# Seven-product k groups in the middle of a pair, and in the out and down projections too

## The chip, the cores and the metric

The kernel runs on one core of one Trainium2 chip. The metric is the device time of one execution in microseconds (us), as a median over several runs. Engines are named as in the profile: PE is TensorE's matmul, PEld its weight load, DVE is VectorE, ACT ScalarE, POOL GpSimd, SP SyncE (here it only issues loads and stores). L494 is line 494 of the kernel before.

## The reference

A decoder trunk of two layers on 256 tokens of width 2048, in float32. Every large product has 256 rows (two tiles of 128 tokens) and a weight that is streamed once from memory.

```
h = h + mamba2_mixer(rmsnorm(h)) # z, x, B, C, dt by in_proj (2048 -> 10304); ends in y @ out_proj (4096 -> 2048)
h = h + swiglu(rmsnorm(h))       # g, u = split(h @ w_gate_up) (2048 -> 2 x 5632); (silu(g) * u) @ w_down (5632 -> 2048)
k, v, cum = shared_kv(h)         # 2048 -> 4112
h = h + forgetting_attention(rmsnorm(h), k, v, cum)   # w_q (2048 -> 2048), softmax, o @ w_o (2048 -> 2048)
h = h + swiglu(rmsnorm(h))       # w_gate_up and w_down of the second layer
```

## The kernel before

**Blocks, k groups, pieces.** A weight is cut into blocks of 512 columns (`NB`) and k groups of 512 rows (`KT` = 4 times 128). One block times one k group is a `Unit`, 1 MB, one load on SP into a `wraw` tile (`RAW` = 3 of these). Float32 is computed from two halves, high and low: ACT makes `whi` by a cast (L247), DVE makes `wlo` = raw - `whi` (L253), and PE runs three matmuls for each 128 x 512 of weight and each 128 tokens (high x high, high x low, low x high; L494 to L496). A unit is split in two pieces of 128 x 1024, each with 12 matmuls. The activations lie in slots, split in the same way (`xT`, one slot for each k group).

**What sets the order.** The program is recorded by `stream` in a fixed order, each engine's queue in that order. Before piece i is multiplied, `split_to(i + SPL)` with `SPL` = 4 puts the splits up to piece i + 3 on ACT and DVE; `whi` and `wlo` have 4 buffers each, so the cast of piece i + 3 waits until PE is done with piece i - 1. Work on results (adding into `h`, norms, transposes into the next slots) is written as generators in `Flow`, which puts it between the pieces by planned costs; `flow.finish` forces what is still open of a task into the queues at once.

**Products of sums.** In the gate and up projections (`ffn_up`, 22 pairs of a gate and an up block over both layers) one k group of four is multiplied as a 2 x 2 block matrix (k halves by gate/up, and k halves by token tile) with seven products in place of eight: `split_cross` and `cross_step`, in the order `Cross.ORDER` = d, g, a, c, e, b, f. A product is one piece of 6 matmuls (L410 to L412), so the group has 42 matmuls in place of 48. Its weight operands are made on DVE in place in the raw tiles (four additions of 128 x 1024, L365) and then split like any other. Of the seven, d, g and f read raw quarters or what was added for them; the additions for later products overwrite a quarter, so they stand behind the split that still reads it:

```
src = {"d": b21, "g": b11, "a": b21, "c": b22, "e": b21, "b": b22, "f": b12}[name]
```

The activation operands of a, c, e and f are sums too (`xS`, made in `sums_of`, L555 to L558, when the slot is filled). Before, the crossed k group is the last one, after the three plain ones of gate and then those of up; products g and b go on in the two PSUM tiles of gate (`acc`), f and a in those of up, d, c and e in tiles of a second pool of four (`mis`), which the transposes use as well. `inline` and `rest` (L617 and on, recorded from L624) combine the products on DVE.

**Out and down projections.** `out_stage` (out projection of either mixer, and down projection of layer 0) and the last loop (down projection of layer 1) run four blocks one after the other with `wide`, all k groups plain: 8 k groups in the Mamba out projection, 11 in the down projections, 4 in the attention's.

Of the kernel before, what the change touches and what calls it, by code (L numbers as in the profile page):

```python
# [9 lines left out]
F32 = mybir.dt.float32  # L10
# [7 lines left out]
P = 128  # L18
# [6 lines left out]
G = 8  # L25
# [9 lines left out]
KT = 4  # L35

# [56 lines left out]
class Flow:  # L93
# [70 lines left out]

class Slot:


    def __init__(self, summed=False):
        self.tile, self.task, self.summed, self.sums = None, None, summed, None
# [10 lines left out]
class Block:  # L180
# [3 lines left out]
    def __init__(self, xs, done, fills=None, wcol=None):  # L184
        self.xs, self.done, self.fills, self.wcol = xs, done, fills, wcol
        self.units, self.ps, self.task = [], None, None
        self.paired, self.stops = False, [KT * len(xs) - 1] * NT


class Cross:  # L190
# [7 lines left out]
    ORDER = "dgacebf"  # L198

    def __init__(self, left, right, units, x, inline, rest_of):  # L200
        self.left, self.right, self.units, self.x = left, right, units, x
        self.inline, self.rest_of = inline, rest_of
        self.ps, self.rest = {}, None
# [3 lines left out]
def kernel(ctx: ExitStack, tc: tile.TileContext, xT_d, x_d, cols_d, rows_d, wdt_d, win_d,  # L207
# [99 lines left out]
    def pair(xs, src_l, src_r, inline, rest, fills):  # L307


        both = []  # L310
        for src in (src_l, src_r):
            b = Block(xs, None, fills if src is src_r else None)
            b.paired = True
            if src is src_r:
                b.stops[1] -= KT
            for kg in range(len(xs) - 1):
                b.units.append(Unit(b, kg, src[kg].rearrange("p (k n) -> p k n", n=NB), NB, [[0, 1], [2, 3]]))
            blocks.append(b)
            both.append(b)
        last = [Unit(None, len(xs) - 1, src[len(xs) - 1].rearrange("p (k n) -> p k n", n=NB), NB, [list(range(KT))])  # L320
                for src in (src_l, src_r)]
        blocks.append(Cross(*both, last, xs[-1], inline, rest))
# [35 lines left out]
    def split_cross(x, name):  # L358
# [24 lines left out]
    def cross_step(x, name, parts):  # L383
# [3 lines left out]
        s = slot_of(x.x)  # L387
        left, right = x.left.ps, x.right.ps
        if name == "d":
            x.rest = phase.tile([P, NB], F32, tag="c4", name=nm("rest"))  # L390
            nc.scalar.copy(out=x.rest, in_=right[1])
            flow.work("A", 0.48)
        own = {"g": left[0], "b": left[1], "f": right[0]}
        if name in own:
            ps = own[name]
        elif name == "a":
            ps = right[1]
        else:
            ps = bank([P, NB])
        x.ps[name] = ps  # L400

        def a_of(part, p):
# [3 lines left out]
            return x.x.sums[:, "acef".index(name), part, p, :]  # L406

        for p in range(2):
            xh, xl = a_of(0, p), a_of(1, p)
            nc.tensor.matmul(ps, lhsT=xh, rhs=hi[:, p, :], start=p == 0 and name not in own, stop=False)  # L410
            nc.tensor.matmul(ps, lhsT=xh, rhs=lo[:, p, :], start=False, stop=False)
            nc.tensor.matmul(ps, lhsT=xl, rhs=hi[:, p, :], start=False, stop=p == 1)  # L412
        x.inline(x, name)
        if name == "b":
            x.left.task = Task(None, None)
            x.left.task.done = x.left.task.evac = True
        if name == "f":
            x.right.task = x.right.fills.task = spawn(x.rest_of(x))
# [3 lines left out]
    def stream(pre_load, pre_split):  # L422
        pieces = []
        for b in blocks:
            pieces += [(b, n) for n in Cross.ORDER] if isinstance(b, Cross) else [(u, ks) for u in b.units for ks in u.pieces]
        units = [u for b in blocks for u in b.units]
# [11 lines left out]
        def split_to(n):  # L438
            for i in range(len(parts), min(n, len(pieces))):
                u, ks = pieces[i]  # L440
                if isinstance(u, Cross):
                    parts[i] = split_cross(u, ks)
                    if ks in "ef":
                        load_to(units.index(u.units["ef".index(ks)]) + 1 + RAW)
# [10 lines left out]
        for i, (u, ks) in enumerate(pieces):  # L455
            if isinstance(u, Cross) and ks == "b":
                cross_step(u, ks, parts[i])
                split_to(i + SPL)
                continue
            split_to(i + SPL)  # L460
            if isinstance(u, Cross):
# [25 lines left out]
            if last or (b.paired and u.kg == 0 and ks[0] == 0):  # L487
                order = [(j, t) for t in range(NT) for j in range(len(ks))]
            for n, (j, t) in enumerate(order):
# [6 lines left out]
                nc.tensor.matmul(b.ps[t], lhsT=xl, rhs=hi[:, j, :], start=False, stop=k == b.stops[t])  # L496
# [3 lines left out]
            if last and not b.paired:  # L500
# [3 lines left out]
        for q in (flow.urgent, flow.mid, flow.lazy):  # L504
            while q:
                flow.finish(q[-1])
                q.popleft()
# [38 lines left out]
    def sums_of(dst, half, ps, wcol):  # L546

        if half == 0:
            dst.sums = slot([P, 4, 2, 2, P], F32R, "xS")
        y = tok("y").rearrange("p (f t) -> p f t", t=T)  # L550
        for f in range(2):
            nc.scalar.activation(y[:, f], ps[:, f, :], AF.Copy, scale=col(wcol + 2 * half + f))
        s = tok("xsum").rearrange("p (n t) -> p n t", t=P)
# [5 lines left out]
        yield A(0.72) + V(0.8)  # L559
        split(dst.sums[:, :, 0, half, :], dst.sums[:, :, 1, half, :], s)  # L560
        yield A(0.6) + V(0.6)

# [28 lines left out]
    def out_stage(xs, w_d, wcol, summed=False):  # L591

        ss = const.tile([P, NT, 4], F32, name=nm("ss"))
        nxt = [Slot(summed and j == 3) for j in range(4)]
# [671 lines left out]
```

## Time and profile before

| | before |
|---|---|
| runs | 2542.09, 2542.38, 2542.40 us, median 2542.38 us |
| profiled execution | 2543.43 us, of which span 2541.7 us |
| granted PE clock, mean | 0.999 |
| PE busy | 2526.5 us (99%), 11638 matmuls |
| PEld, DVE, ACT busy | 82%, 69%, 52% |
| HBM | 189 GB/s over the span |

The span is the time from the first to the last instruction of the profiled execution; the time of a run has some 1.7 us more. Matmuls are pipelined, so a row shows each with 0.39 us though the next starts 0.23 us later: what PE does in a stretch is read from starts, not from busy time.

### The profile page before, as it was taken

The page shows a single profiled execution, that of the slowest core. Times are in us where ns is not written, and L with a number is a line of the kernel's source. Part 1 is how long each engine was busy: PE and PEld are TensorE (multiplying, and loading weights), DVE is VectorE, ACT ScalarE, POOL GpSimd, SP SyncE. Part 2 cuts the span into 40 slices and gives each one's busy share as a digit, 9 for nine tenths or more (in the row PEclk, how much of TensorE's full clock was granted, in tenths as well). Part 3 has the DMA queues.
Part 4 walks back from the last instruction along what each step waited for, and adds up shares of the span by engine and source line. Part 5 has one row for each costly group of instructions (what it writes and reads, how often), then busy time and mean ns, then how long its engine had stood idle before and what let it go on. Part 6 is the DMA issues. An engine that isn't in the chain of part 4 may idle for free.

```text
span 2541.7 us, 29859 instructions
## 1 busy us (share of the span) xinstructions
PE 2526.5 (99%) x11638; PEld 2093.4 (82%) x11638; DVE 1742.4 (69%) x2227; ACT 1325.5 (52%) x1683; POOL 37.7 (1%) x52
## 2 busy tenths in 40 slices
PE   9999999999999999999999999999999999999999
PEld 7888888888888888888888888888888888888887
DVE  6777777755477878787444567775587887876444
ACT  6666565654455545454444556564555555544333
POOL 0000000000000000000000010000000000000000
PEclk9999999999999999999999999999999999999999
DMA  7655455445554655555555555445555564655664
GB/s 262 225 174 180 167 182 199 176 172 191 190 196 168 215 183 199 199 181 200 192 189 194 188 181 203 161 156 181 182 180 202 175 222 166 215 182 200 206 201 139
DMA packets 68317, 481.11 MB, mean 189 GB/s; under 512 B 7600, under 2 KB 8256, under 8 KB 10576
## 3 DMA queue, kind: packets, MB, share of 16 engines
q1 hardware_dynamic: 66672, 468.64, 53.1%
q0 software_dynamic: 1504, 10.57, 1.1%
q8 instruction: 91, 1.49, 0.2%
q14 instruction: 50, 0.41, 0.0%
HBM read 477.00 MB, written 2.18 MB: 189 GB/s over the span
## 4 chain that ended last, share of the span: by engine, by line
PE 90%; DVE 7%; ACT 2%; issue 1%; DMA 0%; SPq 0%; ACTq 0%; DVEq 0%
PE acc L494 28%; PE acc L496 28%; PE acc L495 28%; DVE wlo L253 3%; ACT whi L247 2%; PE mis L530 1%; DVE y L624 1%; PE mis L917 1%; DVE wraw L365 1%; DVE sg L624 1%; DVE d L624 1%; PE mis L787 0%; PE mis L923 0%; PE mis L1022 0%; PE mis L852 0%
## 5 line engine op out<-in xcount | busy, mean ns | idle before, releaser
L253 DVE TENSOR_TENSOR wlo<-wraw,whi 128x1024 fp32r<-128x1024 f32 (+1 forms) x851 | 1027.5, 1220 | 560.5 <-ACT whi L247 554.6
L247 ACT CAST whi<-wraw 128x1024 fp32r<-128x1024 f32 (+1 forms) x854 | 885.5, 1050 | 875.6 <-PE acc L496 790.5
L494 PE MATMUL acc<-whi,xT 128*128 128x512 f32 x3040 | 1196.7, 394 | 9.1 <-DVE y L624 6.8
L495 PE MATMUL acc<-wlo,xT 128*128 128x512 f32 x3040 | 1184.3, 390 | 1.0 <-DVE wlo L253 1.0
L496 PE MATMUL acc<-whi,xT 128*128 128x512 f32 x3040 | 1184.4, 390 | 0.0
L494 PEld LDWEIGHTS acc<-whi,xT 128*128 128x128 f32 x3040 | 571.2, 188 | 134.3 <-DVE y L624 16.1
L496 PEld LDWEIGHTS acc<-whi,xT 128*128 128x128 f32 x3040 | 571.1, 188 | 119.8
L495 PEld LDWEIGHTS acc<-wlo,xT 128*128 128x128 f32 x3040 | 571.6, 188 | 116.8 <-DVE wlo L253 1.6
L255 DVE SCALAR_TENSOR_TENSOR wlo<-wraw,cols,whi 128x512 fp32r<-128x512 f32 x192 | 134.6, 747 | 74.7 <-ACT whi L249 74.0
L249 ACT ACTIVATE whi<-wraw,cols 128x512 fp32r<-128x512 f32 x192 | 127.5, 717 | 73.9 <-PE acc L496 68.8
L253 DVE TENSOR_TENSOR xT<-mis,xT 128x512 fp32r<-128x512 f32 x52 | 33.5, 686 | 38.3 <-ACT xT L247 38.3
L247 ACT CAST xT<-mis 128x512 fp32r<-128x512 f32 x52 | 27.9, 589 | 54.5 <-PE mis L530 54.5
L365 DVE TENSOR_TENSOR wraw<-wraw 128x1024 f32<-128x1024 f32 x44 | 53.9, 1225 | 1.5
L365 DVE TENSOR_TENSOR wraw<-wraw,wraw 128x1024 f32<-128x1024 f32 x44 | 53.9, 1224 | 1.5
L517 POOL TENSOR_TENSOR rs<-ms,mhalf 128x4 f32<-128x4 f32 (+1 forms) x27 | 28.4, 1052 | 1503.2 <-DVE ms L515 1502.9
L494 PE MATMUL acc<-whi,oT 128*128 128x512 f32 x128 | 50.5, 394 | 0.0
L496 PE MATMUL acc<-whi,oT 128*128 128x512 f32 x128 | 49.9, 390 | 0.0
L495 PE MATMUL acc<-wlo,oT 128*128 128x512 f32 x128 | 49.8, 389 | 0.0
L249 ACT ACTIVATE xT<-mis,cols 128x256 fp32r<-128x256 f32 x64 | 25.5, 475 | 35.1 <-PE mis L530 35.1
L255 DVE SCALAR_TENSOR_TENSOR xT<-mis,cols,xT 128x256 fp32r<-128x256 f32 x64 | 26.8, 477 | 22.4 <-ACT xT L249 22.2
L800 DVE SCALAR_TENSOR_TENSOR xf<-mis,cols,xf 128x255 f32<-128x255 f32 (+2 forms) x96 | 39.7, 473 | 2.4 <-ACT xf L794 2.4
L410 PE MATMUL acc<-whi,xT 128*128 128x512 f32 x88 | 34.2, 389 | 0.0
(221 smaller groups left out, 1672.1 us busy)
## 6 DMA issues: line engine op xcount, KB each, us to landing
wraw<-in_gu_dram SPq DMA_DIRECT2D x176, 1024.0 KB, 4.8
wraw<-in_dn_dram SPq DMA_DIRECT2D x88, 1024.0 KB, 4.9
wraw<-in_win_dram SPq DMA_DIRECT2D x78, 1024.0 KB, 4.9
wraw<-in_wout_dram SPq DMA_DIRECT2D x32, 1024.0 KB, 4.8
wraw<-in_wq_dram SPq DMA_DIRECT2D x16, 1024.0 KB, 4.8
wraw<-in_wk_dram SPq DMA_DIRECT2D x16, 1024.0 KB, 4.8
wraw<-in_wv_dram SPq DMA_DIRECT2D x16, 1024.0 KB, 4.8
wraw<-in_wo_dram SPq DMA_DIRECT2D x16, 1024.0 KB, 4.8
```

The lines of the kernel that those rows point to most:

```text
L247: nc.scalar.copy(out=hi, in_=src)
L249: nc.scalar.activation(hi, src, AF.Copy, scale=scal)
L253: nc.vector.tensor_tensor(out=lo, in0=src, in1=hi.bitcast(F32), op=ALU.subtract)
L255: nc.vector.scalar_tensor_tensor(out=lo, in0=src, scalar=scal, in1=hi.bitcast(F32), op0=ALU.mult, op1=ALU.subtract)
L365: nc.vector.tensor_tensor(out=out, in0=in0, in1=in1, op=ALU.add)
L410: nc.tensor.matmul(ps, lhsT=xh, rhs=hi[:, p, :], start=p == 0 and name not in own, stop=False)
L494: nc.tensor.matmul(b.ps[t], lhsT=xh, rhs=hi[:, j, :], start=k == 0, stop=False)
L495: nc.tensor.matmul(b.ps[t], lhsT=xh, rhs=lo[:, j, :], start=False, stop=False)
L496: nc.tensor.matmul(b.ps[t], lhsT=xl, rhs=hi[:, j, :], start=False, stop=k == b.stops[t])
L517: nc.gpsimd.tensor_tensor(out=r, in0=ms, in1=mhalf[:, :width], op=ALU.pow)
L624: nc.vector.tensor_tensor(out=out, in0=in0, in1=in1, op=op)
L800: nc.vector.scalar_tensor_tensor(out=dst[:, i, s:], in0=pt[half][:, f, :T - s], scalar=col(w + 3 - s), in1=dst[:, i, s:], op0=ALU.mult, op ...
```

## The change

The crossed k groups become entries of a pair's common order. `pair` now alternates left and right units by k group and puts a `Group` where a k group is crossed; all products of a pair's crossed groups accumulate in the same seven PSUM tiles, d, a, e and c in four `mis` tiles of their own, and g, b and f in left's two tiles and right's first. They are combined once, at the last group (`parts`, `parts_to_h`). Gate and up have the crossed group at k group 2 of 0 to 3. The Mamba out projection crosses k groups 3 and 6 of 8 in both pairs (`WOUT`), the down projections 3 and 7 (`DN0`) and 3, 6 and 9 (`DN1`) of 11, the attention's out projection 2 of 4. That is 16 crossed groups more, 38 in all. The order of the products becomes d, g, a, e, c, b, f, and one addition moves with it from c to a. The sums for the activations of the new groups are made by `add_sums` from the two halves of a filled slot. Before the first group of a pair, `finish_all` forces all open work into the queues.

```
-    ORDER = "dgacebf"
+    ORDER = "dgaecbf"
...
+WOUT, DN0, DN1 = (3, 6), (3, 7), (3, 6, 9)
...
+    def finish_all(self):
+        for q in (self.urgent, self.mid, self.lazy):
+            while q:
+                self.finish(q[-1])
+                q.popleft()
...
+    def pair(xs, sources, done, fills, crossed, parts):
+        both = [Block(xs, d, f) for d, f in zip(done, fills)]
+        x = Cross(*both, parts)
+        order = []
+        for kg in range(len(xs)):
+            us = [Unit(b, kg, src[kg].rearrange("p (k n) -> p k n", n=NB), NB, [[0, 1], [2, 3]])
+                  for b, src in zip(both, sources)]
+            if kg in crossed:
+                order.append(Group(x, us, xs[kg], kg == crossed[0], kg == crossed[-1]))
+            else:
+                for b, u in zip(both, us):
+                    b.units.append(u)
+                order += us
+        blocks.append(order)
...
         split_hi(hi, src)
         if name == "g":
             add(b22, b12, b22)
-        if name == "c":
-            add(b21, b12, b21)
         split_lo(hi, lo, src)
         if name == "d":
             add(b21, b21, b22)
+        if name == "a":
+            add(b21, b12, b21)
         if name == "c":
             add(b22, b11, b21)
...
+        x, act = group.cross, group.x
+        s = slot_of(act)
+        if act.adder is not None:
+            flow.finish(act.adder)
+        own = {"g": x.left.ps[0], "b": x.left.ps[1], "f": x.right.ps[0]}
+        if group.first:
+            if name == "d":
+                flow.finish_all()
+            x.ps[name] = own[name] if name in own else bank([P, NB])
...
+        if group.last and name == "c":
+            spawn(x.parts(x))
...
-            if isinstance(u, Cross) and ks == "b":
-                cross_step(u, ks, parts[i])
-                split_to(i + SPL)
-                continue
             split_to(i + SPL)
-            if isinstance(u, Cross):
+            if isinstance(u, Group):
                 cross_step(u, ks, parts[i])
...
+    def add_sums(dst):
+        def run():
+            if not dst.task.done:
+                yield dst.task
+            s = dst.tile
+            for half in range(2):
+                y = tok("y").rearrange("p (f t) -> p f t", t=T)
+                part = [s[:, i, 2 * half:2 * half + 2, :].bitcast(F32) for i in range(2)]
+                nc.vector.tensor_tensor(out=y, in0=part[0], in1=part[1], op=ALU.add)
+                yield V(0.66)
+                yield from sums_from(dst, half, y)
+        dst.adder = spawn(run(), flow.mid)
...
+        def gate(x, ps):
+            for t, g in enumerate(x.part[:2]):
+                yield tt(g, ps[t], g)
...
-        for j in range(4):
-            wide(xs, w_d[j], done(j), nxt[j])
+        for j in (0, 2):
+            pair(xs, w_d[j:j + 2], (done(j), done(j + 1)), nxt[j:j + 2], crossed, parts_to_h(j))
```

What the change does to the queues, at three places. Numbers in names tell buffers apart; lines shift with the change (split L253 becomes L266, addition L365 becomes L378, combining L624 becomes L616).

DVE, the crossed group of the sixth gate/up pair of layer 0, before: `wraw_8505` holds the gate's unit (b11, b21), `wraw_8554` the up's (b12, b22). The splits (`wlo`) are those of d, g, a, c, e, b, and after `sg` that of f.

```order
L253 TENSOR_TENSOR wlo_8605<-wraw_8505,whi_8604 128x1024
L365 TENSOR_TENSOR wraw_8505<-wraw_8505,wraw_8554 128x2x512
L365 TENSOR_TENSOR wraw_8554<-wraw_8554 128x2x512
L253 TENSOR_TENSOR wlo_8622<-wraw_8505,whi_8621 128x1024
L253 TENSOR_TENSOR wlo_8639<-wraw_8505,whi_8638 128x1024
L365 TENSOR_TENSOR wraw_8505<-wraw_8554,wraw_8505 128x2x512
L253 TENSOR_TENSOR wlo_8655<-wraw_8554,whi_8654 128x1024
L365 TENSOR_TENSOR wraw_8554<-wraw_8505 128x2x512
L253 TENSOR_TENSOR wlo_8670<-wraw_8505,whi_8669 128x1024
L253 TENSOR_TENSOR wlo_8684<-wraw_8554,whi_8683 128x1024
L624 TENSOR_TENSOR sg_8693<-acc_8428,d_8681 128x512
L253 TENSOR_TENSOR wlo_8696<-wraw_8554,whi_8695 128x1024
```

The same engine in a crossed group of that stage with the change, `wraw_7886` the gate's and `wraw_7926` the up's unit; splits of d, g, a, e, c, b, f:

```order
L266 TENSOR_TENSOR wlo_7992<-wraw_7886,whi_7991 128x1024
L378 TENSOR_TENSOR wraw_7886<-wraw_7886,wraw_7926 128x2x512
L378 TENSOR_TENSOR wraw_7926<-wraw_7926 128x2x512
L266 TENSOR_TENSOR wlo_8009<-wraw_7886,whi_8008 128x1024
L266 TENSOR_TENSOR wlo_8026<-wraw_7886,whi_8025 128x1024
L378 TENSOR_TENSOR wraw_7886<-wraw_7926,wraw_7886 128x2x512
L266 TENSOR_TENSOR wlo_8043<-wraw_7886,whi_8042 128x1024
L266 TENSOR_TENSOR wlo_8054<-wraw_7926,whi_8053 128x1024
L378 TENSOR_TENSOR wraw_7926<-wraw_7886 128x2x512
L266 TENSOR_TENSOR wlo_8067<-wraw_7926,whi_8066 128x1024
L266 TENSOR_TENSOR wlo_8078<-wraw_7926,whi_8077 128x1024
```

The split of e now follows straight behind the addition that makes e's operand, and the split of b straight behind the addition that makes b's; before, another product's split stood in between at both places. The casts on ACT stand in the same order as the splits.

DVE around the end of a gate/up pair, before: `d`, `y` and `u` combine products, `acc_8429` is the gate's second PSUM tile, which the next pair's gate writes again; the splits are those of the next pair's first pieces.

```order
L253 TENSOR_TENSOR wlo_8696<-wraw_8554,whi_8695 128x1024
L253 TENSOR_TENSOR wlo_8709<-wraw_8590,whi_8708 128x1024
L624 TENSOR_TENSOR d_8681<-mis_8712,d_8681 128x512
L624 TENSOR_TENSOR y_8719<-mis_8701,d_8681 128x512
L624 TENSOR_TENSOR y_8719<-y_8719,acc_8429 128x512
L253 TENSOR_TENSOR wlo_8730<-wraw_8590,whi_8729 128x1024
```

And with the change, where the gate's tiles (`acc_7888`, `acc_7889`) are read while PE runs up's last unit, and up's (`acc_7928`, `acc_7929`) while it runs the next gate's first:

```order
L266 TENSOR_TENSOR wlo_8133<-wraw_8058,whi_8132 128x1024
L266 TENSOR_TENSOR wlo_8151<-wraw_8081,whi_8150 128x1024
L266 TENSOR_TENSOR wlo_8167<-wraw_8081,whi_8166 128x1024
L616 TENSOR_TENSOR d_8101<-acc_7888,d_8101 128x512
L616 TENSOR_TENSOR y_8103<-acc_7889,y_8103 128x512
L266 TENSOR_TENSOR wlo_8189<-wraw_8113,whi_8188 128x1024
L266 TENSOR_TENSOR wlo_8205<-wraw_8113,whi_8204 128x1024
L616 TENSOR_TENSOR v_8102<-acc_7928,v_8102 128x512
```

The last product's result moved away from the border of two pairs, by one unit of 24 matmuls on either side.

DVE at the first crossed group of the Mamba out projection, with the change: `wlo_4507` is the split of e, `wlo_4575` that of c. Between them stand four splits of `xT` (slot 7) and four times the six rows from L579 to L266 `xS`, two for slot 3 (`xS_4531`) and two for slot 6 (`xS_4550`); one of the four is shown.

```order
L266 TENSOR_TENSOR wlo_4507<-wraw_4343,whi_4506 128x1024
L268 SCALAR_TENSOR_TENSOR xT_4510<-mis_4511,cols,xT_4510 128x256 x2
L268 SCALAR_TENSOR_TENSOR xT_4510<-mis_4520,cols,xT_4510 128x256 x2
L579 TENSOR_TENSOR y_4529<-xT_3546 128x512
L562 TENSOR_TENSOR xsum_4532<-y_4529 128x128
L563 TENSOR_TENSOR xsum_4532<-y_4529 128x128
L564 TENSOR_TENSOR xsum_4532<-y_4529,xsum_4532 128x128
L565 TENSOR_TENSOR xsum_4532<-y_4529,xsum_4532 128x128
L266 TENSOR_TENSOR xS_4531<-xsum_4532,xS_4531 128x4x128
...
L266 TENSOR_TENSOR wlo_4575<-wraw_4400,whi_4574 128x1024
```

Before, there is only the filling of slot 7 at the same spot, between two plain splits:

```order
L253 TENSOR_TENSOR wlo_4470<-wraw_4341,whi_4469 128x1024
L255 SCALAR_TENSOR_TENSOR xT_4481<-mis_4482,cols,xT_4481 128x256 x2
L255 SCALAR_TENSOR_TENSOR xT_4481<-mis_4491,cols,xT_4481 128x256 x2
L253 TENSOR_TENSOR wlo_4507<-wraw_4398,whi_4506 128x1024
```

So 28 instructions came in between the split of e and that of c, which DVE runs in this order. At the first crossed group of the down projection of layer 1 the last slot's share of these stands at the same spot (one `xS` and two times six rows), at that of layer 0 one `xS`.

## Rows read from the trace of the kernel before

**Rows 1.** Page, part 1: busy time.

```profile
PE 2526.5 (99%) x11638; PEld 2093.4 (82%) x11638; DVE 1742.4 (69%) x2227; ACT 1325.5 (52%) x1683; POOL 37.7 (1%) x52
```

**Rows 2.** Waits of PE: total us, times, longest us.

```profile
PE acc L494 <- DVE y L624: 6.8, 22, 0.9
```

**Rows 3.** Timeline of PE in plain pieces: start us, duration, engine, line, [idle before].

```profile
1100.08 0.39 PE L494 MATMUL acc<-whi,xT 128*128 128x512 f32 x1
...
1108.24 0.39 PE L494 MATMUL acc<-whi,xT 128*128 128x512 f32 x1
```

**Rows 4.** Timeline of PE at the borders of gate/up pairs.

```profile
1138.15 0.39 PE L496 MATMUL acc<-whi,xT 128*128 128x512 f32 x1
1138.77 0.50 PE L494 MATMUL acc<-whi,xT 128*128 128x512 f32 x1 [0.23 <-DVE y L624]
1139.11 0.40 PE L495 MATMUL acc<-wlo,xT 128*128 128x512 f32 x1
...
1182.35 0.50 PE L494 MATMUL acc<-whi,xT 128*128 128x512 f32 x1 [0.91 <-DVE y L624]
...
1862.17 0.50 PE L494 MATMUL acc<-whi,xT 128*128 128x512 f32 x1 [0.58 <-DVE y L624]
```

**Rows 5.** Timeline of PE in one crossed group: d's first matmul, b's second.

```profile
1127.50 0.39 PE L410 MATMUL mis<-whi,xT 128*128 128x512 f32 x1
...
1134.52 0.39 PE L411 MATMUL acc<-wlo,xT 128*128 128x512 f32 x1
```

**Rows 6.** Timeline of ACT in and behind the same group: casts.

```profile
1125.02 1.05 ACT L247 CAST whi<-wraw 128x1024 fp32r<-128x1024 f32 x1 [1.71 <-PE acc L496]
...
1131.42 4.13 ACT L247 CAST whi<-wraw 128x1024 fp32r<-128x1024 f32 x4 [0.71 <-DVE wraw L365]
1137.37 2.00 ACT L247 CAST whi<-wraw 128x1024 fp32r<-128x1024 f32 x2 [1.82 <-DMA wraw<-in_gu_dram]
```

**Rows 7.** Timeline of DVE in the same group, from the split of a on.

```profile
1126.11 1.22 DVE L253 TENSOR_TENSOR wlo<-wraw,whi 128x1024 fp32r<-128x1024 f32 x1 [0.60 <-ACT whi L247]
1127.36 1.22 DVE L365 TENSOR_TENSOR wraw<-wraw,wraw 128x1024 f32<-128x1024 f32 x1
...
1130.09 1.22 DVE L365 TENSOR_TENSOR wraw<-wraw 128x1024 f32<-128x1024 f32 x1
1131.23 2.50 DVE L253 TENSOR_TENSOR wlo<-wraw,whi 128x1024 fp32r<-128x1024 f32 x2
```

**Rows 8.** DMA issues: operation xcount, KB each, median us to landing.

```profile
wraw<-in_gu_dram SPq DMA_DIRECT2D x176, 1024.0 KB, 4.8
```

**Rows 9.** Timeline of DVE and ACT, operations on slots and sums.

```profile
554.00 1.66 DVE L255 SCALAR_TENSOR_TENSOR xT<-mis,cols,xT 128x256 fp32r<-128x256 f32 x4
...
707.66 0.84 ACT L249 ACTIVATE xT<-mis,cols 128x256 fp32r<-128x256 f32 x2 [2.11 <-PE mis L530]
...
710.32 0.29 DVE L555 TENSOR_TENSOR xsum<-y 128x128 f32<-128x128 f32 x1 [0.91 <-ACT y L552]
...
711.05 0.29 DVE L558 TENSOR_TENSOR xsum<-y,xsum 128x128 f32<-128x128 f32 x1
...
711.38 0.62 ACT L247 CAST xS<-xsum 128x512 fp32r<-128x512 f32 x1 [0.15 <-DVE xsum L558]
```

**Rows 10.** Groups of DVE and ACT: sum's split, an addition of 128 x 512, row sums.

```profile
L253 DVE TENSOR_TENSOR xS<-xsum,xS 128x512 fp32r<-128x512 f32 x4 | 2.7, 681 | 0.0
L951 DVE TENSOR_TENSOR xs<-xs,zs 128x512 f32<-128x512 f32 x16 | 10.4, 684 | 0.0
L521 ACT ACTIVATE junk<-h 128x512 f32<-128x512 f32 x24 | 15.1, 639 | 0.0
```

**Rows 11.** Start of the kernel: timeline of PE; windows (us; busy (x); PEclk, DMA share, GB/s).

```profile
12.46 0.79 PE L495 MATMUL acc<-wlo,xT 128*128 128x512 f32 x1 [0.76 <-DVE wlo L253]
...
15.57 0.40 PE L496 MATMUL acc<-whi,xT 128*128 128x512 f32 x1
...
10.00:16.00 6.00, 4.04 (x10) 3.04 (x11) 4.95 (x8) 5.52 (x9) 0.00 (x0) 0.72 1.03 423
```

More of the change, by code (lines that the diff above doesn't have):

```diff
@@ L186, in __init__ @@
         self.units, self.ps, self.task = [], None, None
-        self.paired, self.stops = False, [KT * len(xs) - 1] * NT
 class Cross:
-    ORDER = "dgacebf"
[L200 to L203, printed above, removed]
+    ORDER = "dgaecbf"
+    def __init__(self, left, right, parts):
+        self.left, self.right, self.parts, self.ps = left, right, parts, {}
+class Group:
+    def __init__(self, cross, units, x, first, last):
+        self.cross, self.units, self.x, self.first, self.last = cross, units, x, first, last
 @with_exitstack
@@ L381, in split_cross, with cross_step @@
         return hi, lo, ready
-    def cross_step(x, name, parts):
+    def cross_step(group, name, parts):
         hi, lo, ready = parts
         flow.work("E", 0.0, ready)
[L387 to L400, printed above, removed]
+        x, act = group.cross, group.x
[7 more added lines that the diff above has]
+            x.ps[name] = own[name] if name in own else bank([P, NB])
+        ps = x.ps[name]
         def a_of(part, p):
@@ L405, in a_of @@
                 return s[:, part, 2 * p + k, t * P:(t + 1) * P]
-            return x.x.sums[:, "acef".index(name), part, p, :]
+            return act.sums[:, "acef".index(name), part, p, :]
         for p in range(2):
             xh, xl = a_of(0, p), a_of(1, p)
-            nc.tensor.matmul(ps, lhsT=xh, rhs=hi[:, p, :], start=p == 0 and name not in own, stop=False)
+            nc.tensor.matmul(ps, lhsT=xh, rhs=hi[:, p, :], start=group.first and p == 0 and name not in own, stop=False)
             nc.tensor.matmul(ps, lhsT=xh, rhs=lo[:, p, :], start=False, stop=False)
[L412 to L418, printed above, removed]
+            nc.tensor.matmul(ps, lhsT=xl, rhs=hi[:, p, :], start=False, stop=group.last and p == 1 and name not in own)
+        if group.last and name == "c":
+            spawn(x.parts(x))
         flow.work("E", STEP)
@@ L486, in stream @@
             order = [(j, t) for j in range(len(ks)) for t in range(NT)]
[L487 removed]
+            if last:
                 order = [(j, t) for t in range(NT) for j in range(len(ks))]
@@ L499, in stream @@
                     flow.pump()
-            if last and not b.paired:
+            if last:
                 b.task = spawn(b.done(b.ps))
@@ L503, in stream @@
                     b.fills.task = b.task
[L504 to L507, printed above, removed]
+        flow.finish_all()
     def rsqrt_of(ss, n, width):
@@ new lines, in up @@
+        def up(x, ps, nb):
+            g, s = x.part[:2], x.part[2:]
+            for t in range(NT):
+                yield tt(s[t], ps[t], s[t])
+            yield EVAC
+            for t in range(NT):
+                nc.vector.scalar_tensor_tensor(out=s[t], in0=s[t], scalar=r[0][:, t:t + 1], in1=g[t], op0=ALU.mult, op1=ALU.mult)
+                yield V(0.66)
+            yield SYNC
+            yield from to_slot(acts[nb], lambda t, f: s[t][:, f * P:(f + 1) * P], None)
+            if nb == NFB - 1:
+                for kg in summed:
+                    add_sums(acts[kg])
@@ L669, in ffn_up, with took @@
+        for nb in range(NFB):
+            x = [None]
+            def took(y, x=x):
+                x[0] = y
+                return parts(y)
+            pair(xs, gu_d[2 * nb:2 * nb + 2], (lambda ps, x=x: gate(x[0], ps), lambda ps, x=x, nb=nb: up(x[0], ps, nb)),
+                 (None, acts[nb]), (2,), took)
         return acts
@@ L1170, in final @@
         return run
-    for j in range(4):
-        wide(act1, dn1_d[j], final(j))
+    for j in (0, 2):
+        pair(act1, dn1_d[j:j + 2], (final(j), final(j + 1)), (None, None), DN1, parts_to_h(j))
     pre_load = {i: (lambda i=i: load_x(i)) for i in range(4)}
```

143 lines of the change are left out of this document (67 added, 76 removed).

## The prediction

> **What bounds the kernel now.** I read the page's busy times first, since they say whose steps are the time: PE is busy 99% of the span [rows 1]. The list of PE's waits then says how little it stands [rows 2]: 6.8 us at the 22 borders of gate/up pairs, where a combining addition is late. So time is matmuls times the step between them, plus stalls. The step is read from starts, not from the durations shown: 36 matmuls between 1100.08 and 1108.24 [rows 3], 8.16 / 36 = 0.2267 us. A piece of 12 is 2.72 us, a product of 6 is 1.36, a crossed group 9.52, the plain pair of units that it replaces 10.88. ACT and DVE, at 52% and 69%, have room on the whole; whether a single piece's operand is ready in time is another question, and this change turns on it.
>
> **The change part by part.**
>
> *Matmuls.* 16 more crossed groups times 6 matmuls: 96 fewer, 96 x 0.2267 = **-21.8 us**, if nothing stalls.
>
> *Pair borders.* At a border, 1138.15 to 1139.11 holds two steps [rows 4]: 0.62 to the waiting matmul, then 0.34 for the one behind it, 0.96 where 0.45 would do. That is 0.5 us, 22 times 11.0. Three borders stand longer: idle 0.91 twice and 0.58 once against 0.23, 0.7 + 0.7 + 0.35. With the change gate's tiles are read while PE runs up's last unit (5.4 us), so this wait goes: **-12.7 us**. Three combining operations of 0.68 stand among the splits there; they must fit in what is free, and by the splits' 1.22 us [rows 7] they do, by a few tenths only.
>
> *The order a, e, c, b.* This is what costs. I count from d's start on PE, 1127.50 [rows 5], and take gaps and durations from ACT and DVE in the same group [rows 6, 7]. The cast of a starts when PE frees a `whi` buffer, at -2.48 (1125.02), and its split at -1.39 (1126.11). In both kernels an addition stands behind the split of a, from -0.14 to 1.08 (1127.36, 1.22 us); in the row of before it is recorded in c, and its place on DVE is the same.
>
> Before, c's split comes next, then the addition for b (1130.09 to 1131.31), then the splits of e and b, one row of two, 1131.23 to 1133.73. b's second matmul, the first that needs the low half, runs at 1134.52: b is 0.8 us early.
>
> Now e comes next. Its cast can't start before the addition ends plus 0.11 (as 1131.42 follows 1131.31): 1.19 to 2.24. Split of e 2.27 to 3.49; e needs it at 4.31 (third product's end, 4.08, and one step). Split of c, whose cast ran meanwhile, 3.41 to 4.63 (an operation that waits for nothing starts 1.14 after the one before it, as 1131.23 follows 1130.09); c needs it at 5.67. Addition for b, 4.66 to 5.88. Cast of b 5.99 to 7.04. Split of b 7.07 to 8.29, and its second matmul at 8.34. It was due at 1134.52 - 1127.50 = 7.02. PE stands 1.32, and the step behind a stall is 0.34 in place of 0.23 [rows 4], 0.11 more: **1.43 us for each crossed group**. Nothing takes it back: f is ready at 9.5, when PE, late by now, comes to it, and the next casts hang on PE's own progress. A crossed group then takes 9.52 + 1.43 = 10.95 us, as long as the plain units. All 38 pay it, the 22 old ones too: 38 x 1.43 = **+54.3 us**. Bounds: 0 if the casts come earlier than I chain them (below), 2.5 if an addition and a split more stand in the chain (2 x 1.22).
>
> *Loads.* A load takes 4.8 us [rows 8]. Before, the left unit's buffer came free with e's split, 1132.4, and a cast waited for its load until 1137.37 [rows 6], 9.9 after d, for a piece that PE starts at 15.0 (two pieces behind the group's 9.52): PE felt nothing. Now the buffer comes free with the addition in c, 5.88, and 4.9 later is 10.8, for a piece that starts at 16.4; cast and split take 2.5 of the 5.6 between. So nothing, hidden behind the two pieces of the plain unit; without that cover a late load costs what it is late, 0.9 us a group here.
>
> *Work forced out at a pair's first group.* `finish_all` stands at d, after the split of e, so what is open is put on DVE and ACT between the split of e and that of c. An `xS` half costs: its addition 0.68, like another of 128 x 512 [rows 10]; four `xsum` from 710.32 to 711.34, 1.02; the cast 0.62, 0.04 later [rows 9]; its split 0.68 [rows 10]. They follow each other: 3.04.
> - Mamba out projection, first pair: four `xT` operations 1.66 [rows 9] and four halves 12.2, 13.8 in all. From 3.53 that puts the split of c at 17.4 to 18.6, the addition to 19.8, the cast of b to 21.0, its split to 22.25. b's second matmul: 22.3. It was due at 7.02, or 7.9 with the slot's transposes on PE, which stand in both kernels (an estimate of four steps): 14.4 late, less the 1.32 counted already, and three refills of 0.11: +13.4.
> - Down projection of layer 1: one split of `xS` and two halves, 0.68 + 6.08 = 6.8, with refills +7.1. Of layer 0, one split: +0.6.
> - First gate/up pair of either layer: four `xT` on ACT (0.84 for two) and two row-sum passes of 0.64 stand ahead of the cast of a [rows 9, 10], 3.0 us, so it starts at 0.5, not -2.48. The chain above, shifted, gives b's second matmul at 11.3 in place of 8.34; with two refills +3.2, twice 6.4.
>
> Together **+27.5**. Bounds: 0, if ACT and DVE had run this before d (the queues' order speaks against it, but sources may be ready early), and about 35, with 0.5 more for each half.
>
> *Sum.* -21.8 - 12.7 + 54.3 + 27.5 = +47.3. The profiled execution's span is 2541.7, so 2589; a run has some 0.7 to 1.7 us more and the median of the runs was 2542.4: **2590 us**.
>
> **The rivals.**
>
> *Nothing stalls at b (faster).* The price of 1.43 rests on a chain of six operations. It decides at 1.3 us: were the split of b done by 7.0, all of it would be gone. What speaks for it: before, the same operations ended 0.8 us early, and DVE is 69% busy. Against it: before, c's split lay between e's addition and e's split, and e's between b's addition and b's split, so the cast's 1.05 us on ACT was covered; now DVE stands twice waiting for a cast. Then it is -21.8 - 12.7 + 27.5 = -7.0, 2535; without the forced work 2508. The Trainium skill, "Perfetto Trace Analysis", section "Identifying the Most-Contended Engine", says to work on the engine with the highest occupancy first, and for TensorE to judge by weight loads rather than matmul time; both point at PE here, so by that rule fewer matmuls would bring the gain. The trace agrees as to which engine, and shows no stall of this kind that the rule could weigh.
>
> *The stall alone.* The forced work is over before the group, or fits into idle time: -21.8 - 12.7 + 54.3 = +19.8, about 2562. For it: those slots' sources are done some time ahead. Against: it stands in the queue where the change's rows on DVE put it, between the splits of e and c.
>
> *PE falls to its lower clock at each stall.* At the kernel's start PE waited 0.76 for a split, and the 8 matmuls from 12.46 to 15.57 took 3.11 us where full speed gives 1.81 [rows 11], at a granted clock of 0.72 in that stretch, so between the levels of 1.2 and 2.4 GHz: 1.3 us lost. At 38 stalls that is +49, 2640. Against it: PE waits 22 times at borders [rows 2], up to 0.91 us [rows 4], and the steps of rows 3, 5 us behind one such border (a pair is 43.6 long, 1138.77 to 1182.35), are at full speed; at the kernel's start PE had done little before. The Trainium skill, "TensorE: Matmul & The Clock Gate", section "A second HAM failure mode: psum-queue depth-cycling", tells of short idle times between groups of matmuls that let the gate swing. By it this rival would be the forecast; the trace's 22 borders don't bear it out so far.
>
> **How the numbers follow.** Own forecast 0.69; the stall alone 0.15; no stall at b 0.11; clock 0.05. Own range: the stall at 1.0 to 1.9 (a quarter to either side and more) and the forced work at 15 to 35 give 2570 to 2612. The range over the cases reaches down to take in the stall alone and up by 24 for a bigger stall, and leaves out the faster case and the clock: 2557 to 2614. A measurement tells 0.2%, 5 us, from no change. Faster by more: the 0.11. Within it: 0.03, cut from the lower flank of the stall alone and the forecast. Slower: 0.86.
>
> **What would show it.** In the list of PE's waits, a new entry of some 38 for DVE's split at the second matmul of b, 1.2 to 1.4 us each, and no more of the 22 waits on a combining addition at a border: right. A crossed group's starts spanning 9.5 us with no idle: the faster rival. One gap of some 13 us in all (c, then b) in the Mamba out projection's first pair, 7 in that of layer 1's down projection, 3 in the first gate/up pairs: the forced work; none of them: the stall alone. 11542 matmuls; a mean granted clock well below 0.99: the clock. The forecast is wrong if the chain has an overlap that I did not see, above all if the cast of b or e starts before the addition ahead of it ends, or if loads come late at every group.

## The result, and the profile after

| | after |
|---|---|
| runs | 2626.01, 2626.03, 2627.15, 2628.31 us, median 2626.59 us |
| profiled execution | 2626.01 us, of which span 2624.2 us |
| ratio to before | 1.0331, 95% interval 1.0313 to 1.0349 |
| granted PE clock, mean | 0.992 |

The kernel became slower by 84 us; the forecast was 48 slower, and its range ended at 2614. One execution of the last experiment's kernel, e9_perpair, took 4056.17 us at a mean granted clock of 0.581 and is left out of the medians and ratios below. The page of the changed kernel, busy times and the row of granted clock (40 slices of the span; 9 is 90% of full speed or more):

```profile
PE 2543.8 (97%) x11542; PEld 2080.6 (79%) x11542; DVE 1941.1 (74%) x2499; ACT 1366.4 (52%) x1733; POOL 38.1 (1%) x52
...
PEclk9999999989999999999999999999999999999999
```

The 96 matmuls are gone, and PE's share fell from 99% to 97% [rows 1]: what was saved went into waits. The clock dips in the ninth slice, 525 to 590 us. The list of PE's waits (total us, times, longest us) says into which; before, the largest entry was 6.8 us on a combining addition [rows 2]. Its first six:

```profile
PE acc L420 <- DVE wlo L266: 28.0, 38, 0.8
PE acc L500 <- DVE h L616: 16.8, 3, 8.2
PE mis L419 <- ACT whi L260: 8.1, 4, 4.9
PE acc L419 <- ACT whi L260: 7.6, 35, 0.8
PE mis L419 <- ACT xS L260: 6.3, 2, 4.8
PE acc L500 <- ACT zs L981: 3.3, 1, 3.3
```

The first and the fourth are the stall of b in the crossed groups, 38 times. (The idle time listed is less than what a stall costs, which is read from starts below.) The third and the fifth are the first groups of a stage. The second and the last are new, and the forecast had no place for them: PE waits at the start of a plain block (L500) for an addition into `h`, and once for a `zs` of the z projection. The waits at the 22 borders of gate/up pairs are gone.

**A regular crossed group.** Timelines of PE (d's first matmul, b's first and second, and the first plain matmul behind the group), of ACT and of DVE in the crossed group from 1116.56 on:

```profile
1116.56 0.39 PE L419 MATMUL mis<-whi,xT 128*128 128x512 f32 x1
...
1123.67 0.50 PE L419 MATMUL acc<-whi,xT 128*128 128x512 f32 x1 [0.15 <-ACT whi L260]
1124.93 0.50 PE L420 MATMUL acc<-wlo,xT 128*128 128x512 f32 x1 [0.76 <-DVE wlo L266]
...
1127.56 0.39 PE L500 MATMUL acc<-whi,xT 128*128 128x512 f32 x1
```

```profile
1114.08 1.05 ACT L260 CAST whi<-wraw 128x1024 fp32r<-128x1024 f32 x1 [1.71 <-PE acc L502]
1117.76 2.00 ACT L260 CAST whi<-wraw 128x1024 fp32r<-128x1024 f32 x2 [2.62 <-DVE wraw L378]
1122.58 2.94 ACT L260 CAST whi<-wraw 128x1024 fp32r<-128x1024 f32 x3 [2.82 <-DVE wraw L378]
```

```profile
1116.42 1.22 DVE L378 TENSOR_TENSOR wraw<-wraw,wraw 128x1024 f32<-128x1024 f32 x1
1118.84 2.36 DVE L266 TENSOR_TENSOR wlo<-wraw,whi 128x1024 fp32r<-128x1024 f32 x2 [1.19 <-ACT whi L260]
1121.24 1.23 DVE L378 TENSOR_TENSOR wraw<-wraw 128x1024 f32<-128x1024 f32 x1
1123.65 3.50 DVE L266 TENSOR_TENSOR wlo<-wraw,whi 128x1024 fp32r<-128x1024 f32 x3 [1.19 <-ACT whi L260]
```

Read from d's start: cast of e at 1.20, its split at 2.28, the addition for b at 4.68, the cast of b at 6.02, its split at 7.09, b's second matmul at 8.37. Twice DVE stands 1.19 us for a cast, which in turn waits for the addition that DVE has just made. The group takes 1127.56 - 1116.56 = 11.00 us, 1.48 more than its 42 steps of 0.2267. Worked out in this way, from d's start to the start of the first plain matmul behind, 31 of the 38 groups read between 1.4 and 1.6 over.

**The border behind an out projection.** PE, DVE and ACT where the Mamba out projection ends and the first gate/up pair begins (PE runs gate's first unit from 722 to 728):

```profile
736.92 0.76 PE L500 MATMUL acc<-whi,xT 128*128 128x512 f32 x1 [8.21 <-DVE h L616]
737.49 0.63 PE L501 MATMUL acc<-wlo,xT 128*128 128x512 f32 x1
737.91 0.63 PE L502 MATMUL acc<-whi,xT 128*128 128x512 f32 x1
...
740.46 0.40 PE L502 MATMUL acc<-whi,xT 128*128 128x512 f32 x1
```

```profile
726.41 0.88 DVE L268 SCALAR_TENSOR_TENSOR xT<-mis,cols,xT 128x256 fp32r<-128x256 f32 x2 [1.61 <-ACT xT L262]
728.19 0.29 DVE L562 TENSOR_TENSOR xsum<-y 128x128 f32<-128x128 f32 x1 [0.91 <-ACT y L553]
...
733.78 0.29 DVE L562 TENSOR_TENSOR xsum<-y 128x128 f32<-128x128 f32 x1 [0.90 <-ACT y L553]
...
735.49 0.69 DVE L266 TENSOR_TENSOR xS<-xsum,xS 128x512 fp32r<-128x512 f32 x1 [0.68 <-ACT xS L260]
736.10 1.28 DVE L616 TENSOR_TENSOR h<-h,acc 128x512 f32<-128x512 f32 x2
```

The last row empties the right block's two PSUM tiles into `h`. These tiles were complete at 722, and up's first piece needs them again, one unit of 5.4 us later. But on DVE the additions stand behind the whole filling of the left block's slot with its sums, a chain that goes to and fro between PE, ACT and DVE. PE stands for 8.21 us, and the eight steps behind take 740.46 - 736.92 = 3.54 us where 1.81 would do. That is 10 us, and the same border behind the attention's out projection, at 1880, costs the same.

**The first group of the Mamba out projection.** DVE in one of the four sum halves between the splits of e and c:

```profile
566.83 0.68 DVE L579 TENSOR_TENSOR y<-xT 128x512 f32<-128x512 f32 x1
567.54 0.29 DVE L562 TENSOR_TENSOR xsum<-y 128x128 f32<-128x128 f32 x1
...
569.25 0.69 DVE L266 TENSOR_TENSOR xS<-xsum,xS 128x512 fp32r<-128x512 f32 x1 [0.68 <-ACT xS L260]
569.86 0.68 DVE L579 TENSOR_TENSOR y<-xT 128x512 f32<-128x512 f32 x1
```

A half takes 569.86 - 566.83 = 3.03 us. The group goes from 561.52 to 588.08 on PE, 26.56 us, 17.0 over its steps. PE's first wait in it is at a, whose activation operand is one of the forced sums:

```profile
569.27 0.50 PE L419 MATMUL mis<-whi,xS 128*128 128x512 f32 x1 [4.77 <-ACT xS L260]
```

### The profile page after: what moved, and what is told of

Its sections match the earlier page's. It is cut to its first block, busy times and chain, and to the rows that moved or that the text cites. A ratio compares the mean times of both kernels' runs of the same rounds, so it can differ in the third digit from the quotient of the medians.

```text
span 2624.2 us, 30058 instructions
## 1 busy us (share of the span) xinstructions
PE 2543.8 (97%) x11542; PEld 2080.6 (79%) x11542; DVE 1941.1 (74%) x2499; ACT 1366.4 (52%) x1733; POOL 38.1 (1%) x52
## 4 chain that ended last, share of the span: by engine, by line
PE 60%; DVE 13%; ACT 6%; issue 1%; ACTq 0%; POOL 0%; DVEq 0%
PE acc L500 18%; PE acc L501 18%; PE acc L502 18%; DVE wlo L266 8%; ACT whi L260 5%; DVE wraw L378 4%; PE acc L420 2%; PE acc L421 1%; PE mis L533 1%; PE acc L419 1%; DVE xT L268 0%; PE mis L1066 0%; PE mis L1134 0%; ACT xT L262 0%; PE mis L1157 0%
## 5 line engine op out<-in xcount | busy, mean ns | idle before, releaser
L266 DVE TENSOR_TENSOR wlo<-wraw,whi 128x1024 fp32r<-128x1024 f32 (+1 forms) x899 | 1077.0, 1220 | 451.8 <-ACT whi L260 446.2
L260 ACT CAST whi<-wraw 128x1024 fp32r<-128x1024 f32 (+1 forms) x902 | 925.0, 1047 | 846.4 <-PE acc L502 500.7
L500 PE MATMUL acc<-whi,xT 128*128 128x512 f32 x2816 | 1110.4, 394 | 21.6 <-DVE h L616 16.8
L501 PE MATMUL acc<-wlo,xT 128*128 128x512 f32 x2816 | 1101.4, 391 | 0.8 <-DVE wlo L266 0.8
L502 PE MATMUL acc<-whi,xT 128*128 128x512 f32 x2816 | 1099.3, 390 | 0.0
L500 PEld LDWEIGHTS acc<-whi,xT 128*128 128x128 f32 x2816 | 530.7, 188 | 134.0 <-ACT junk L524 17.4
L502 PEld LDWEIGHTS acc<-whi,xT 128*128 128x128 f32 x2816 | 530.4, 188 | 110.6
L419 PE MATMUL mis<-whi,xS 128*128 128x512 f32 x228 | 90.9, 399 | 14.4 <-ACT whi L260 8.1
L378 DVE TENSOR_TENSOR wraw<-wraw,wraw 128x1024 f32<-128x1024 f32 x76 | 93.1, 1225 | 2.6
L378 DVE TENSOR_TENSOR wraw<-wraw 128x1024 f32<-128x1024 f32 x76 | 93.1, 1225 | 2.6
L420 PE MATMUL mis<-wlo,xS 128*128 128x512 f32 x228 | 91.0, 399 | 2.7 <-DVE wlo L266 2.7
L421 PE MATMUL mis<-whi,xS 128*128 128x512 f32 x228 | 90.8, 398 | 0.0
L420 PE MATMUL acc<-wlo,xT 128*128 128x512 f32 x144 | 61.2, 425 | 26.8 <-DVE wlo L266 26.8
L419 PE MATMUL acc<-whi,xT 128*128 128x512 f32 x144 | 61.1, 424 | 7.2 <-ACT whi L260 7.2
L419 PEld LDWEIGHTS mis<-whi,xS 128*128 128x128 f32 x228 | 43.6, 191 | 26.2 <-ACT whi L260 10.1
L420 PEld LDWEIGHTS acc<-wlo,xT 128*128 128x128 f32 x144 | 27.5, 191 | 43.0 <-DVE wlo L266 38.4
L266 DVE TENSOR_TENSOR xT<-mis,xT 128x512 fp32r<-128x512 f32 x52 | 33.5, 686 | 34.5 <-ACT xT L260 34.4
L421 PE MATMUL acc<-whi,xT 128*128 128x512 f32 x144 | 57.4, 398 | 0.0
```

Source lines behind the costliest of these rows:

```text
L260: nc.scalar.copy(out=hi, in_=src)
L266: nc.vector.tensor_tensor(out=lo, in0=src, in1=hi.bitcast(F32), op=ALU.subtract)
L378: nc.vector.tensor_tensor(out=out, in0=in0, in1=in1, op=ALU.add)
L419: nc.tensor.matmul(ps, lhsT=xh, rhs=hi[:, p, :], start=group.first and p == 0 and name not in own, stop=False)
L500: nc.tensor.matmul(b.ps[t], lhsT=xh, rhs=hi[:, j, :], start=k == 0, stop=False)
L501: nc.tensor.matmul(b.ps[t], lhsT=xh, rhs=lo[:, j, :], start=False, stop=False)
```

## The experiments

The theory after the result: three losses, each of an order in a queue. (1) Casts of e and b wait for an addition right ahead of them. (2) At a pair's end the right block's PSUM tiles are read behind the left block's slot. (3) Sums are forced in at a pair's first group. The rival to all three is that DVE, at 74%, simply has too much to do near the groups, so that a loss removed in one place comes back in another. Each kernel was timed beside the kernel before; the medians of before lay between 2542.7 and 2543.1 us.

| run | edit | median, us | ratio to before |
|---|---|---|---|
| e1_order | old order of products | 2560.9 | 1.0073 (1.0058 to 1.0088) |
| e2_border | right block's additions at once | 2606.7 | 1.0257 (1.0240 to 1.0274) |
| e3_later | first groups later | 2619.2 | 1.0295 (1.0279 to 1.0310) |
| e4_all | these three together | 2530.5 | 0.9949 (0.9934 to 0.9964) |
| e5_nonew | changed kernel, no new groups | 2595.1 | 1.0204 (1.0189 to 1.0220) |
| e6_46 | e4_all, groups 4 and 6 | 2528.8 | 0.9942 (0.9925 to 0.9958) |
| e7_46z | e6_46, z tiles at once | 2523.8 | 0.9923 (0.9909 to 0.9938) |
| e8_nonew_all | e4_all, no new groups | 2538.5 | 0.9981 (0.9972 to 0.9991) |
| e9_perpair | e7_46z, first pair crosses 6 alone | 2515.7 | 0.9891 (0.9871 to 0.9911) |

**The order (e1_order).**

```
-    ORDER = "dgaecbf"
+    ORDER = "dgacebf"
...
+        if name == "c":
+            add(b21, b12, b21)
         split_lo(hi, lo, src)
...
-        if name == "a":
-            add(b21, b12, b21)
```

With it the combination starts at e, and the left unit's buffer is loaded again from e on, not from c.

> The changed kernel with the order of the products d, g, a, c, e, b, f of before, and the addition for e again ahead of the split of c. Own theory (each of 38 groups loses 1.47 us at the second matmul of b, because casts of e and b wait for an addition right ahead of them): 38 x 1.48 = 56 us go, 2626.6 to about 2570, and the groups that are not the first of a stage's first pair take 9.5 us with no idle. Rival (DVE has too much to do in a group, eleven operations of 1.22 us in 9.5 us, whatever their order): PE still waits in each group, and the time stays above 2610.

2560.9, 66 us less. PE and DVE in a regular group of that run (d's first matmul, b's second, the first behind the group; the addition for b and the splits of e, b and the two pieces behind):

```profile
1093.95 0.39 PE L419 MATMUL mis<-whi,xT 128*128 128x512 f32 x1
...
1100.97 0.39 PE L420 MATMUL acc<-wlo,xT 128*128 128x512 f32 x1
...
1103.47 0.39 PE L500 MATMUL acc<-whi,xT 128*128 128x512 f32 x1
```

```profile
1096.54 1.23 DVE L378 TENSOR_TENSOR wraw<-wraw 128x1024 f32<-128x1024 f32 x1
1097.68 4.78 DVE L266 TENSOR_TENSOR wlo<-wraw,whi 128x1024 fp32r<-128x1024 f32 x4
```

b's second matmul is back at 7.02 and the group at 9.52 us; DVE runs the same eleven operations with no idle time between the addition and four splits. So the stall is the order's and not DVE's load. The gain is 10 us larger than 38 x 1.48. The five first groups sum to 26 us over in place of 38 (Mamba out 16.0 for 17.0, layer 1's down 7.3 for 10.7, the first gate/up pairs 1.4 each for 4.8 and 3.7, layer 0's down 0 for 2.1), which is 5 more than the 5 x 1.48 already counted. Another 6 lie between the groups: 2 ahead of the first one, most of it a granted clock that fell behind the wait for `zs` in the one trace and not in the other (last section), and 4 in pieces of at most 0.5 that I have not followed.

**The border (e2_border).** For the right block of a pair whose products go into `h`, the task is advanced past its two additions as soon as its last piece is recorded (this holds for layer 0's down projection too):

```
                 b.task = spawn(b.done(b.ps))
...
+                while b.eager and not b.task.evac:
+                    flow.advance(b.task)
```

> The changed kernel, but the two additions into h that empty the right block's PSUM tiles at the end of the Mamba and the attention's out projections are put on DVE at once, ahead of the left block's transposes and sums. Own theory (the next up's first piece needs these tiles 5.4 us after their last matmul, and the additions stand 8 us behind the left block's slot): both gaps of 8.4 us at 737 and 1880 go, with the slow steps behind them, 10 us each: about 2606. Rival (the gap is the combination of the products ahead, or the row sums; the additions only come last): gaps of 5 us or more stay, 2618 or above.

2606.7, as expected. DVE at the same border:

```profile
720.33 1.28 DVE L620 TENSOR_TENSOR h<-h,acc 128x512 f32<-128x512 f32 x2
721.52 1.22 DVE L267 TENSOR_TENSOR wlo<-wraw,whi 128x1024 fp32r<-128x1024 f32 x1
722.66 1.28 DVE L620 TENSOR_TENSOR h<-h,acc 128x512 f32<-128x512 f32 x2
723.85 1.22 DVE L267 TENSOR_TENSOR wlo<-wraw,whi 128x1024 fp32r<-128x1024 f32 x1
```

The right block's additions now stand at 722.66, one split behind the left block's, and of PE's 16.8 us of waits on `h` 0.4 are left. Little came back: the first gate/up groups lose 6.7 and 5.2 us in place of 4.8 and 3.7.

**First groups later (e3_later).** `WOUT` from (3, 6) to (5, 6), `DN1` from (3, 6, 9) to (5, 7, 9).

> The changed kernel with the crossed k groups of the Mamba out projection at 5 and 6 (not 3 and 6) and of layer 1's down projection at 5, 7 and 9 (not 3, 6 and 9): as many matmuls and groups. Own theory (what finish_all forces into the first group is the loss there; 17.0 and 10.5 us in these two groups, against 1.5 in another): later groups find the sums made, so 15.5 + 9 = 24 us go: about 2602; 2615 if half of it is still forced. Rival (the first group of a stage costs this wherever it stands): 2626.

A miss: 2619.2, 7 less and not 24. The two first groups did shrink, from 17.0 to 1.8 and from 10.7 to 1.5 us over, 24 together, so what was forced in made them long, and not that they come first. But the second crossed group of the Mamba out projection, now right behind the first, went from 1.5 to 6.2 over in both pairs, and three of the later ones in layer 1's down projection, two k groups apart now, to 2.5, 2.7 and 3.3; why these three lose more is not shown. The groups are read from an execution of 2613.1 us; the other three took 2619.2 to 2619.7, at a mean granted clock of 0.993 to 0.994 for 0.995.

**All three (e4_all).**

> The three edits of the other runs together (old order, right block's additions at once, later first groups). Own theory, if the three losses add up: 2626.6 - 56 - 20 - 24 = about 2527, so faster than before (2542.4) by 15; what stays is 5 us at the first gate/up pairs and 5 at the start of the Mamba out projection. Rival (a loss removed in one place comes back in another, since DVE then is the limit): above 2542.

2530.5, faster than before by 12 us. The losses add up: one by one the edits gained 66, 20 and 7 us, and all three 96. So DVE's load is not the limit. What is left shows why adjacent groups lose; DVE between the two groups of the first pair:

```profile
586.62 4.77 DVE L267 TENSOR_TENSOR wlo<-wraw,whi 128x1024 fp32r<-128x1024 f32 x4
593.06 1.22 DVE L380 TENSOR_TENSOR wraw<-wraw,wraw 128x1024 f32<-128x1024 f32 x1 [1.67 <-DMA wraw<-in_wout_dram]
```

The addition recorded behind d's split (it makes a's operand) takes both units of the second group, and the right one has not landed: with three raw buffers, two of them are held by the group before until it is nearly done. The split of g stands behind that addition, and PE waits 2.57 us for it (at 596.73). By an estimate from these rows 1.67 of the 2.57 are the late load, and 0.9 would stay without it. The steps behind, at a granted clock of 0.50, make most of the other 2 us of the 4.7 that this group loses.

**Without the new groups (e5_nonew, e8_nonew_all).** `WOUT`, `DN0` and `DN1` empty, and none in the attention's out projection; the first on the changed kernel, the second with the old order and the additions at once.

> The changed kernel without the 16 new crossed groups: out and down projections in pairs, but all their k groups plain; the 22 gate/up groups as changed. Own theory (each new group loses 1.47 us for 1.36 gained, the first ones of the Mamba out projection and of layer 1's down projection 17.0 and 10.5): 2626.6 + 21.8 - 23.5 - 15.5 - 9.1 - 0.6 = about 2600, so the new groups lose 27 us in all; and the gaps of 8.4 us at the two borders stay, since they come from pairing and not from crossing. Rival (the new groups do bring their gain, the loss is elsewhere): 2640 or above; and if the combinations make the border gaps, these are gone.

> The old order and the right block's additions at once, and no new crossed groups: what pairing and own banks alone bring. Own theory: of before's 2542.4 the 22 borders give back 12, the start of the Mamba out projection costs 5 and the first gate/up groups 4: 2539, at most 2544; the 16 new groups then are worth 9 to 15 us in the run with all edits. Rival (the new groups are worth nothing even there, since sums cost what matmuls save): 2530.

2595.1 and 2538.5. In the changed kernel the 16 new groups cost 2626.6 - 2595.1 = 31 us. In the mended one they are worth 2538.5 - 2530.5 = 8 us, near the lower end of what was expected, and pairing with banks of its own for each product is worth some 4. The border without any crossing, PE in e5_nonew:

```profile
717.11 0.77 PE L500 MATMUL acc<-whi,xT 128*128 128x512 f32 x1 [6.20 <-DVE h L616]
```

It stays, 2 us shorter than with crossing, so it comes from pairing.

**Groups apart, and the z block (e6_46, e7_46z).** `WOUT` at (4, 6); then also the last z block's tiles emptied at once, by the same two lines as at the border.

> The three edits together, with the Mamba out projection's groups at 4 and 6 in place of 5 and 6. Own theory (in two crossed groups right behind each other DVE gets 22 operations of 1.22 us in 19 us, and a plain group between gives it time to catch up): the 4.7 and 4.4 us that the second group loses in either pair go, 2530.5 to about 2522, if the sums are made by k group 4; 2528 if they are half forced there. Rival (those losses are work of the slots or the sums, not adjacency): 2530.

> As the run with groups at 4 and 6, and the last z block's PSUM tiles are emptied on ACT at once, ahead of the gating of the block before. Own theory (same cause as at the other borders: the right block of the first pair needs these tiles 5.4 us after their last matmul): the 3.4 us gap at 531 and its slow steps go, 4 to 5 us under that run, about 2518. Rival (ACT is held up by other work there in any order): no change.

2528.8: the second groups read 9.5 us in both pairs, so the loss was adjacency. I had expected it from the number of DVE's operations; the rows of e4_all show a late load as its larger part. The gain went back into the first group at 4, 9.2 us over, since two sum halves are still forced there. In that group PE waits for a cast that stands on ACT behind them:

```profile
584.16 0.80 PE L421 MATMUL mis<-whi,xS 128*128 128x512 f32 x1 [6.13 <-ACT whi L261]
```

2523.8 with the z tiles at once, 5 less, as expected; the wait on `zs` is gone. In the traces 3.8 us of it lie ahead of the first group; that group loses 7.2 in place of 9.2, and a late one in layer 1's down projection 1.1 more.

**One group in the first pair (e9_perpair).** The first pair of the Mamba out projection crosses 6 alone, the second 3 and 6.

> As the run with the z block's tiles emptied at once, but the first pair of the Mamba out projection crosses only k group 6 and the second pair 3 and 6; the sum for 6 is made first. Own theory (the 7.2 us that the first group at 4 still loses are two sum halves forced between two splits; by k group 6 they are made): 7.2 less go, 1.4 for six matmuls more come: 2523.8 - 5.8 = 2518. Rival (a pair's first group loses this wherever it stands, for instance to the forced order itself): 2525.

2515.7, 1.1% faster than before, and 2 us better than expected. Page, first lines:

```profile
span 2514.6 us, 30065 instructions
...
PE 2503.5 (100%) x11548; PEld 2077.5 (83%) x11548; DVE 1930.6 (77%) x2492; ACT 1368.0 (54%) x1730; POOL 39.9 (2%) x52
```

Of 37 groups 34 read 9.52 us, and the others lose 4.9 us together; DVE at 77% is busier than in the changed kernel, and the list of PE's waits has 4.4 us for it in all.

## Why the prediction was wrong

The direction and the main mechanism were right; the sum was short by 35 us of span (82.5 measured, 47.3 forecast).

- **Matmuls, -21.8:** 96 fewer, as said.
- **The order a, e, c, b, +54.3:** right, by its own steps. 1.48 us for 1.43 forecast; b's second matmul at 8.37 for 8.34, the cast of b at 6.02 for 5.99. Shown by e1_order.
- **Work forced out, +27.5:** right in kind, somewhat small. Over and above the regular 1.48: Mamba out 15.5 (13.4), layer 1's down 9.2 (7.1), the first gate/up pairs 3.3 and 2.2 (3.2 each), layer 0's down 0.6 (0.6), 31 in all. The half took 3.03 (3.04), and in the Mamba group b's second matmul came at 22.7 (22.3). What was missing is the clock: in the wake of these waits PE ran at its lower level (below), 6.4 us in three of the groups, and the forecast priced only the waits. Two readings were off without much effect: the first wait came at a and not at c, since a needs a forced sum too, and the slot's transposes stand ahead of the group (560.73 to 561.52), so b was due at 7.0 and not 7.9.
- **Pair borders, -12.7: the step that failed.** For the 22 borders between gate/up pairs it held; their waits are gone. But I asked only when gate's tiles are read. The right block's tiles have the same short time, one unit of 5.4 us, at every border where a pair follows, also behind an out projection and behind the z projection. There the read stands behind other work in the same queue: 10 us at 737, 10 at 1880, 5 at 531 (3.3 of wait, the rest slow steps behind it), together 25 that the sum had at nothing. Before, a block's tiles had a whole block's time to be read. e2_border and e7_46z show it, e5_nonew that pairing does it.
- **Loads, 0:** right for this change, in which the list of PE's waits names no load; a late load was found only where two groups adjoin (e4_all).
- What stays open: some 5 us of the 82.5 are spread over the span in pieces that I have not followed; 4 of them go with the old order (e1_order).
- **The sums:** the range was cut a little short by its own terms, since a stall of 1.9 and 35 of forced work give 72.2 + 35 - 34.5 = 72.7 us, 2615 and not 2612. In the clock rival 12.46 to 15.57 holds seven steps and not eight, so 1.5 us a stall and not 1.3. Neither changes the outcome.

Of the rivals, "nothing stalls at b" and "the stall alone" fell with the first profile. The clock rival is answered from windows of the changed kernel (us, busy and count of PE, PEld, DVE, ACT, POOL, granted clock, DMA share, GB/s):

```profile
565.00:590.00 25.00, 15.18 (x39) 9.99 (x40) 19.98 (x37) 9.95 (x13) 0.00 (x0) 0.73 0.27 92
736.92:740.05 3.13, 3.13 (x8) 2.45 (x9) 0.45 (x1) 0.00 (x0) 0.00 (x0) 0.50 0.00 0
767.70:771.06 3.36, 3.36 (x9) 2.58 (x8) 3.33 (x5) 2.41 (x3) 0.00 (x0) 0.51 0.89 293
1116.56:1127.56 11.00, 10.09 (x44) 7.80 (x42) 8.58 (x8) 6.38 (x7) 0.00 (x0) 1.00 0.37 108
```

The regular group with its two short stalls keeps a granted clock of 1.00, so that rival fell for the regular groups, which are all but seven. Behind the 8.21 us wait the clock is 0.50, which is 1.2 GHz, for eight steps. In the first gate/up group behind that border PE waited 0.24, 0.77, 0.75 and 0.77 us between 760 and 767, and its last steps ran at 0.51; the same group of layer 1, with four waits within 0.01 us of these, kept 1.00. Steps near 0.43 us cost 2.8, 1.2 and 2.4 us in three of the first groups and 1.4 at each of the three borders, 10.6 in all. So the lower clock had a real price, but all of it except those 1.2 us stands behind waits of over 3 us, and none in the 31 regular groups. The Trainium skill, "TensorE: Matmul & The Clock Gate", section "A second HAM failure mode: psum-queue depth-cycling", lets short idle times between groups swing the gate; in this trace 0.15 and 0.76 us, in those 31 groups, did not, and for them the measurement decides; the four waits of a first gate/up group were followed by a fall in one of two places.

## What to carry to other kernels

When an operand is made by one engine, cast by a second and subtracted on the first again, the order must put another product's work between the steps; three dependent neighbours in the queues turned 9.5 us into 11.0, with PE, ACT and DVE each idle for part of it. When two accumulators end one unit apart in place of one block apart, list every place where their banks are needed again and what stands ahead of the read in its queue, at the ends of stages first. And a saving that first shows as a loss can be real: with the queues mended, 16 groups, four of them at later k groups, gave 8 us.

## What the runs showed of the hardware that I had not expected

The same wait did not always bring the clock down. PE's wait of 3.27 us for `zs` stands in eight of the traces, and the granted clock fell to 0.50 with it or up to 1.6 us behind it in four (the changed kernel, e4_all, e6_46, e8_nonew_all); in the others (e1_order, e2_border, e3_later, e5_nonew) the next steps stay at full speed. Windows behind it in the changed kernel, where seven steps took 0.43 us, and in e1_order:

```profile
532.43:535.42 2.99, 2.99 (x9) 2.34 (x8) 0.00 (x0) 0.14 (x1) 0.60 (x1) 0.50 0.95 312
530.45:536.00 5.55, 5.55 (x24) 4.60 (x25) 2.21 (x3) 3.42 (x6) 0.69 (x1) 1.00 0.57 189
```

Behind both waits of 8.21 us it had already fallen at the first matmul. The fall thus added 1.7 us to a wait of 8 at each of the two out-projection borders, and 1.4 or nothing to a wait of 3.3: what a wait costs can differ by this much between two executions, in a place that no edit touched. What decides it, no row here shows.
